# Group softmax: the last columns of three stores go out in ranges of partitions

One core of a Trainium2 chip. The metric is device time of the whole kernel in microseconds (us). Before the change it was 1326.43 us, the median of runs between 1326.30 and 1326.44.

## The reference

```python
def setup_inputs():
    B, N, D, G = 4, 4096, 4352, 8
    return {"x": np.random.randn(B, N, D).astype(np.float32)}

def reference(x):
    B, N, D = x.shape
    x_g = x.reshape(B, N, 8, D // 8)
    x_g = x_g - x_g.max(axis=-1, keepdims=True)
    exp = np.exp(x_g)
    return (exp / exp.sum(axis=-1, keepdims=True)).reshape(B, N, D)
```

285 MB are read and 285 MB written; there is little arithmetic for each byte.

## The kernel before

The input is cut into `nt` = 64 tiles of 128 partitions by 8704 columns of float32 (34,816 B per partition). There are six tile buffers. SyncE issues the loads. VectorE takes the maxima, ScalarE the exponentials and sums, VectorE multiplies by the reciprocals. GpSimdE issues the stores of tiles 0 to 61, SyncE the last two. A load of tile `t` waits until the store of tile `t - 6` has freed its buffer.

```python
    for t in range(nt):                                  # SyncE: loads
        if t >= NT:
            nc.sync.wait_ge(stored[t % NT], 16 * (t // NT))
        ...
            nc.sync.dma_start(out=tile_in[:, :], in_=xt[t]).then_inc(landed[t % NT], 16)
    ...
    for t in range(nt - LAST, nt):                       # SyncE: the last two stores
        nc.sync.wait_ge(scaled, t + 1 if t < nt - 1 else len(parts))
        nc.sync.dma_start(out=ot[t], in_=bufs[t % NT][:, :]).then_inc(last_stored, 16)

    for t in range(nt - LAST):                           # GpSimdE: all other stores
        nc.gpsimd.wait_ge(scaled, t + 1)
        nc.gpsimd.dma_start(out=ot[t], in_=bufs[t % NT][:, :]).then_inc(stored[t % NT], 16)
```

Of the kernel before, what the change touches and what calls it, by code (L numbers as in the profile page):

```python
# [1 line left out]

# [4 lines left out]


@with_exitstack
def kernel(  # L10
    ctx: ExitStack,
    tc: tile.TileContext,
    x: bass.AP,
    out: bass.AP,
):
    nc = tc.nc
    G = 8
    P = 128
    R = 2
    NT = 6  # L20
    RG = R * G
    xf = x.flatten_outer_dims()
    of = out.flatten_outer_dims()
    N, D = xf.shape
    Dg = D // G
    nt = N // (P * R)
    LAST = 2
    FIRST = 2
    turns = (nt - 1 - FIRST) // NT
    f32 = mybir.dt.float32  # L30
    X = mybir.AxisListType.X
    Exp = mybir.ActivationFunctionType.Exp
    xt = xf.rearrange("(t p r) d -> t p (r d)", p=P, r=R)
    ot = of.rearrange("(t p r) d -> t p (r d)", p=P, r=R)

    landed = [tc.alloc_semaphore(f"landed{b}") for b in range(NT)]
    stored = [tc.alloc_semaphore(f"stored{b}") for b in range(NT)]
    last_landed = tc.alloc_semaphore("last_landed")
    last_stored = tc.alloc_semaphore("last_stored")


    max_done = tc.alloc_semaphore("max_done")
    exp_done = tc.alloc_semaphore("exp_done")
    rec_done = tc.alloc_semaphore("rec_done")
    scaled = tc.alloc_semaphore("scaled")

    ctx.enter_context(tc.tile_critical(  # L47
        sync_engine=mybir.EngineType.Pool, no_gpsimd_drain=True))
    bufs = [ctx.enter_context(nc.sbuf_tensor(f"xt{b}", [P, R * D], f32)) for b in range(NT)]
    mx = ctx.enter_context(nc.sbuf_tensor("mx", [P, NT, RG], f32))  # L50
    sm = ctx.enter_context(nc.sbuf_tensor("sm", [P, NT, RG], f32))
    rs = ctx.enter_context(nc.sbuf_tensor("rs", [P, NT, RG], f32))

    parts = [(t, slice(0, RG)) for t in range(nt - 1)]
    parts += [(nt - 1, slice(r * G, (r + 1) * G)) for r in range(R)]

    def groups(t, g):
        return bufs[t % NT][:, :].rearrange("p (g d) -> p g d", d=Dg)[:, g, :]

    def vector_max(n):  # L60
        t, g = parts[n]
        i = nc.vector.reduce_max(  # L62
            out=mx[:, t % NT, g], in_=groups(t, g), axis=X, negate=True)
        if g.start == 0:
            i.wait_op(landed[t % NT], 16 * (t // NT + 1), "sem-ge")
        else:
            i.wait_op(last_landed, 16, "sem-ge")
        i.then_inc(max_done, 1)

    def vector_scale(n):  # L70
        t, g = parts[n]
        nc.vector.reciprocal(out=rs[:, t % NT, g], in_=sm[:, t % NT, g]).wait_op(  # L72
            exp_done, n + 1, "sem-ge").then_inc(rec_done, 1)
        xg = groups(t, g)
        nc.vector.tensor_tensor(  # L75
            out=xg,
            in0=xg,
            in1=rs[:, t % NT, g].unsqueeze(2).to_broadcast([P, g.stop - g.start, Dg]),
            op=mybir.AluOpType.mult,
        ).wait_op(rec_done, n + 1, "sem-ge").then_inc(scaled, 1)  # L80

    def scalar_exp(n, count):
        t, gs = parts[n]
        xg = groups(t, gs)
        for g in range(gs.start, gs.stop):
            i = nc.scalar.activation(  # L86
                out=xg[:, g - gs.start, :],
                in_=xg[:, g - gs.start, :],
                func=Exp,
                bias=mx[:, t % NT, g:g + 1],  # L90
                scale=1.0,
                accum_out=sm[:, t % NT, g:g + 1],
            )
            if g == gs.start:
                i.wait_op(max_done, count, "sem-ge")
        i.then_inc(exp_done, 1)



    for t in range(nt):  # L100
        if t >= NT:
            nc.sync.wait_ge(stored[t % NT], 16 * (t // NT))
        tile_in = bufs[t % NT]
        if t < nt - 1:
            nc.sync.dma_start(out=tile_in[:, :], in_=xt[t]).then_inc(landed[t % NT], 16)  # L105
        else:
            for r in range(R):
                nc.sync.dma_start(
                    out=tile_in[:, r * D:(r + 1) * D], in_=xt[t, :, r * D:(r + 1) * D],
                ).then_inc(landed[t % NT] if r < R - 1 else last_landed, 16)  # L110
    for t in range(nt - LAST, nt):
        nc.sync.wait_ge(scaled, t + 1 if t < nt - 1 else len(parts))
        nc.sync.dma_start(out=ot[t], in_=bufs[t % NT][:, :]).then_inc(last_stored, 16)


    for t in range(nt - LAST):
        nc.gpsimd.wait_ge(scaled, t + 1)
        nc.gpsimd.dma_start(out=ot[t], in_=bufs[t % NT][:, :]).then_inc(stored[t % NT], 16)  # L118
    for t in range(nt - NT, nt - LAST):
        nc.gpsimd.wait_ge(stored[t % NT], 16 * (t // NT + 1))  # L120
    nc.gpsimd.drain()
    nc.gpsimd.wait_ge(last_stored, 16 * LAST)

    nc.scalar.preload_act_table(Exp)  # L124

    for n in range(FIRST):
        scalar_exp(n, n + 1)
    nc.scalar.sem_inc(max_done, -FIRST)
    with nc.scalar.Fori(0, turns):
        for k in range(NT):  # L130
            scalar_exp(FIRST + k, k + 1)
        nc.scalar.sem_inc(max_done, -NT)
    for k, n in enumerate(range(FIRST + turns * NT, len(parts))):
        scalar_exp(n, k + 1)


    vector_max(0)
    for n in range(len(parts)):
        if n + 1 < len(parts):
            vector_max(n + 1)  # L140
        vector_scale(n)


# [1 line left out]
_INS = ['x']  # L145
_OUTS = [((4, 4096, 4352), 'float32')]


# [23 lines left out]
```

## Time and profile before

| | before |
|---|---|
| time, median | 1326.43 us |
| span of the profiled execution | 1324.7 us |
| share of 16 DMA engines held by the two queues | 51.5% + 48.3% |
| VectorE, ScalarE busy | 90%, 57% |

The prediction shows the lines and how they are read.

- **Mean and last landing.** The last store (tile 63) has 16 landings in the trace, one for each DMA engine (the packet records string into 16 chains, and in a chain a semaphore packet follows every eight rows of a whole store). The span is the mean of these 16 landings, plus the lag of the last behind the mean, plus 1.39 us, which is the same in the kernel before, the changed kernel and all experiments but two (e11 6.04, e12 9.43). Before: 1320.95 + 2.31 + 1.39 = 1324.65. Rebalancing can only reduce the 2.31.
- **Packets.** An undisturbed packet takes 36.8 ps per byte and 8 ns (1288 ns for 34,816 B).

### The profile page before, as it was taken

What the parts mean: (1) busy time and instruction counts of PE and PEld (TensorE: products, weight loads), DVE (VectorE), ACT (ScalarE), POOL (GpSimd) and SP (SyncE); (2) the same over time, 40 slices, a digit from 0 to 9 for tenths busy, and PEclk for the clock granted to TensorE, in tenths of its full rate; (3) what the DMA queues carried; (4) which work ended last, traced back from release to release, by engine and by line L of the source; (5) the groups of instructions that cost most, each with busy time, mean ns of one, the idle gap of its engine ahead of it and who ended that gap; (6) DMA issues with size and microseconds to landing.
All of it is one profiled execution on the core that took longest, in us unless ns stands there. A gap on an engine that the chain in (4) does not pass through costs nothing.

```text
span 1324.7 us, 2465 instructions
## 1 busy us (share of the span) xinstructions
DVE 1190.0 (90%) x195; ACT 757.4 (57%) x2049; POOL 33.3 (3%) x66
## 2 busy tenths in 40 slices
DVE  5999999988989889898898998988989889898893
ACT  3765566547456465564655646556465474654751
POOL 0000000000000000000000000000000000000000
DMA  9999999999999999999999999999999999999998
GB/s 404 421 434 433 432 432 434 434 432 431 435 435 432 430 434 437 432 432 432 436 434 430 433 435 433 431 433 435 433 433 431 434 436 432 431 432 437 432 432 372
DMA packets 18582, 570.48 MB, mean 431 GB/s; under 512 B 2064, under 2 KB 2064, under 8 KB 2064
## 3 DMA queue, kind: packets, MB, share of 16 engines
q1 hardware_dynamic: 9648, 294.13, 51.5%
q0 software_dynamic: 8928, 276.30, 48.3%
q14 instruction: 6, 0.05, 0.0%
HBM read 285.21 MB, written 285.21 MB: 431 GB/s over the span
## 4 chain that ended last, share of the span: by engine, by line
another core or an unknown queue 69%; DVE 20%; DMA 7%; ACT 1%; SPq 1%; issue 0%; POOLq 0%
DVE xt L75 10%; DVE mx L62 10%; DMA out_dram<-xt 4%; DMA xt<-in_x_dram 3%; ACT xt L86 1%; SPq L105 1%; DVE rs L72 0%; SPq L167 0%; POOLq L47 0%; POOLq L156 0%
## 5 line engine op out<-in xcount | busy, mean ns | idle before, releaser
L86 ACT ACTIVATE xt<-xt,mx 128x544 f32<-128x544 f32 x1024 | 750.1, 734 | 542.4 <-DVE mx L62 542.4
L62 DVE TENSOR_REDUCE mx<-xt 128x16 f32<-128x8704 f32 (+1 forms) x65 | 590.1, 9079 | 110.8 <-DMA xt<-in_x_dram 110.8
L75 DVE TENSOR_TENSOR xt<-xt,rs 128x8704 f32<-128x8704 f32 (+1 forms) x65 | 590.6, 9086 | 2.2
L86 ACT ACTIVATION_READ_ACCUMULATOR xt<-xt,mx 128x1 f32 x1024 | 191.6, 187 | 0.0
L118 POOL DMA_DIRECT2D out_dram<-xt x62 | 33.1, 534 | 1243.5 <-DVE xt L75 1243.5
L72 DVE RECIPROCAL rs<-sm 128x16 f32<-128x16 f32 (+1 forms) x65 | 15.7, 242 | 2.8 <-ACT xt L86 2.8
L124 ACT ACT_TABLE_LOAD x1 | 1.3, 1283 | 0.9 <-PEq L156 0.9
L156 POOL MEMSET const-float32-0.0<- 128x1 f32 x1 | 0.1, 98 | 0.2 <-issue 0.2
L156 POOL MEMSET const-bfloat16-1.0<- 128x1 bf16 x1 | 0.1, 101 | 0.0
L156 POOL MEMSET const-uint8-127<- 128x1 uint8 x1 | 0.1, 99 | 0.0
L156 POOL MEMSET const-float32-1.0<- 128x1 f32 x1 | 0.1, 98 | 0.0
## 6 DMA issues: line engine op xcount, KB each, us to landing
xt<-in_x_dram SPq DMA_DIRECT2D x63, 4352.0 KB, 32.4
out_dram<-xt POOLq DMA_DIRECT2D x62, 4352.0 KB, 51.5
out_dram<-xt SPq DMA_DIRECT2D x2, 4352.0 KB, 20.1
xt<-in_x_dram SPq DMA_DIRECT2D x2, 2176.0 KB, 35.1
```

What stands on the lines that cost most here:

```text
L62: i = nc.vector.reduce_max(out=mx[:, t % NT, g], in_=groups(t, g), axis=X, negate=True)
L72: nc.vector.reciprocal(out=rs[:, t % NT, g], in_=sm[:, t % NT, g]).wait_op(exp_done, n + 1, "sem-ge").then_inc(rec_done, 1)
L75: nc.vector.tensor_tensor(out=xg, in0=xg, in1=rs[:, t % NT, g].unsqueeze(2).to_broadcast([P, g.stop - g.start, Dg]), op=mybir.AluOpType.mu ...
L86: i = nc.scalar.activation(out=xg[:, g - gs.start, :], in_=xg[:, g - gs.start, :], func=Exp, bias=mx[:, t % NT, g:g + 1], scale=1.0, accum ...
L105: nc.sync.dma_start(out=tile_in[:, :], in_=xt[t]).then_inc(landed[t % NT], 16)
L118: nc.gpsimd.dma_start(out=ot[t], in_=bufs[t % NT][:, :]).then_inc(stored[t % NT], 16)
L124: nc.scalar.preload_act_table(Exp)
L156: nc = _bacc.Bacc("TRN2", target_bir_lowering=False, num_devices=1)
```

## The change

The intent, as its form tells it: take work from the DMA engine that ends last. In stores 24, 48 and 56 the last columns of all 128 rows are sent separately, in ranges of unequal numbers of partitions.

```diff
+    ranged = {24: (7344, [5, 105, 18]), 48: (7344, [8, 120]), 56: (8576, [48, 65, 15])}
+
+    def stores_of(t):
+        if t not in ranged:
+            return [(slice(0, P), slice(0, R * D))]
+        col, sizes = ranged[t]
+        dmas, p = [(slice(0, P), slice(0, col))], 0
+        for size in sizes:
+            dmas.append((slice(p, p + size), slice(col, R * D)))
+            p += size
+        assert p == P
+        return dmas
+
+    def stored_count(t):
+        return 16 * sum(len(stores_of(u)) for u in range(t % NT, t + 1, NT))
...
-            nc.sync.wait_ge(stored[t % NT], 16 * (t // NT))
+            nc.sync.wait_ge(stored[t % NT], stored_count(t - NT))
...
-        nc.gpsimd.dma_start(out=ot[t], in_=bufs[t % NT][:, :]).then_inc(stored[t % NT], 16)
+        for ps, cs in stores_of(t):
+            nc.gpsimd.dma_start(out=ot[t, ps, cs], in_=bufs[t % NT][ps, cs]).then_inc(
+                stored[t % NT], 16)
```

More of the change, by code (lines that the diff above doesn't have):

```diff
@@ L117 @@
         nc.gpsimd.wait_ge(scaled, t + 1)
-        nc.gpsimd.dma_start(out=ot[t], in_=bufs[t % NT][:, :]).then_inc(stored[t % NT], 16)
+        for ps, cs in stores_of(t):
+            nc.gpsimd.dma_start(out=ot[t, ps, cs], in_=bufs[t % NT][ps, cs]).then_inc(
+                stored[t % NT], 16)
     for t in range(nt - NT, nt - LAST):
-        nc.gpsimd.wait_ge(stored[t % NT], 16 * (t // NT + 1))
+        nc.gpsimd.wait_ge(stored[t % NT], stored_count(t))
     nc.gpsimd.drain()
```

## The prediction

> **What bounds the kernel now.** I read the page first: the busy shares, the DMA slices and the queues.
>
> ```profile
> DVE 1190.0 (90%) x195; ACT 757.4 (57%) x2049; POOL 33.3 (3%) x66
> DMA  9999999999999999999999999999999999999998
> GB/s 404 421 434 433 432 432 434 434 432 431 435 435 432 430 434 437 432 432 432 436 434 430 433 435 433 431 433 435 433 433 431 434 436 432 431 432 437 432 432 372
> q1 hardware_dynamic: 9648, 294.13, 51.5%
> q0 software_dynamic: 8928, 276.30, 48.3%
> ```
>
> VectorE has a tenth of its time free. The 16 DMA engines do not: the two queues hold 51.5 + 48.3 = 99.8% of their time, and only the first two slices and the last stand visibly below some 433 GB/s. Then the waits, of the engines and of SyncE's queue:
>
> ```profile
> DVE mx L62 <- DMA xt<-in_x_dram: 110.8, 51, 13.9
> SPq L105 <- DMA out_dram<-xt: 1201.7, 57, 67.8
> ```
>
> VectorE's waits are for loads; the loads' issuer waits for stores to free a buffer. Everything waits for transfers. The issues say how deep the transfers queue:
>
> ```profile
> xt<-in_x_dram SPq DMA_DIRECT2D x63, 4352.0 KB, 32.4
> out_dram<-xt POOLq DMA_DIRECT2D x62, 4352.0 KB, 51.5
> ```
>
> A tile's load and store together take some 20.6 us of all 16 engines (the pieces of the chain of waits come every 20.6 us). A load is under way for 32.4 us and a store for 51.5, so each engine always has packets of both waiting, and a late semaphore leaves no engine empty. Last, the end, in narrow stretches (columns: stretch, length, busy time of VectorE, ScalarE, GpSimdE, clock, DMA share, GB/s; a packet is counted where it starts):
>
> ```profile
> 1318.70:1320.00 1.30, 0.00 (x0) 0.00 (x0) 0.00 (x0) 1.00 0.74 321
> 1320.00:1320.60 0.60, 0.00 (x0) 0.00 (x0) 0.00 (x0) 1.00 0.14 58
> 1320.60:1321.50 0.90, 0.00 (x0) 0.00 (x0) 0.00 (x0) 1.00 0.18 77
> 1321.50:1322.00 0.50, 0.00 (x0) 0.00 (x0) 0.00 (x0) 1.00 0.00 0
> ```
>
> A packet is one row of 34,816 B. 58 GB/s over 0.60 us is one packet, 77 over 0.90 two. So three engines begin their last packet after the other 13, and the last of them ends the kernel.
>
> The trace's single packet records show more. On one engine a 34,816 B packet starts 1285 ns after the one before, so the packets can be strung into 16 chains. The chains end, in us from the span's start, at 1319.8 to 1320.8 (12 of them), 1321.1, 1321.3, **1322.2 and 1322.8**; the mean is 1320.6. The chain that is last (S1) loses a few ns on many packets: the last landing of a load falls behind the first by 2.2 us in mid-run and by 3.9 at the end, and from 600 us on the lag grows by 0.3 us every six tiles. The second (S2) was already a packet behind at 100 us, after a start in which the first packets took 1.8 to 2.4 us, and has one instruction fetch of 0.3 us. Were the bytes spread so that all chains ended together, the end would come 1322.8 - 1320.6 = 2.2 us earlier, 0.17%. **That is all that rebalancing can win.**
>
> [...]
> - [...] The trace before has only 128-partition stores, 16 landings each (62 x 16 + 67 x 16 = 2064)[...].
> - [...] in a chain q0 and q1 largely alternate.
> - [...] 16 x 34,816 B / 1285 ns = 433.5.
> - [...]
>
> **The change part by part.** No arithmetic, no load and no byte is taken away. Three of 62 stores (24, 48, 56) become one store of all rows' first columns plus two or three of the last columns. The tails are (8704 - 7344) x 4 = 5440 B per row in stores 24 and 48, (8704 - 8576) x 4 = 512 B in 56.
>
> [...]
>
> *The cost of a byte and a packet*: 34,816 B take 1285 ns and the 17,408 B packets of the last load 645 (start to start), so 36.8 ps per byte and 5 ns per packet. A semaphore packet adds some 6 ns.
> [...]
>
> *Beside it*: GpSimdE issues 8 more DMAs at 0.53 us (33.1 us for 62), 4.3 us, in an engine that waits 1243.5 us for VectorE: hidden. SyncE waits for 64 or 48 instead of 16 semaphore counts a little longer; the queues hide that.
>
> *The sum, if S1 is the relieved engine*: S1 ends at 1322.8 - 2.3 = 1320.5. S2 then sets the end, at 1322.2 + 0.2 to 0.4 = 1322.4 to 1322.6: a gain of only 0.2 to 0.4 us. If S2's early slip is this execution's accident, the next chain is 1321.3 + 0.4 = 1321.7: a gain of 1.1 us.
>
> **The rivals.**
> 1. *The relief misses* ([...]another slow engine in timed runs). For: nothing before shows an engine's number. Against: so exact a pattern must have been measured. The end moves by the +0.2 to +0.4 us that the others get: 1326.7.
> 2. [...] Tails of 24 and 48 are 8 x 5440 B x 36.8 ps = 1.6 us per engine each; a quarter to a half lost on both is +0.8 to +1.6 us, which cancels the gain: 1326.5 to 1328. For: the opening packets of up to 2.4 us[...]. Against: from there on almost all take 1288 ns, with loads and stores mixed.
> 3. *All lag goes*: both slow chains are nearer to the others in timed runs, and the whole 2.2 us less some 0.3 is won: 1324.5.
> 4. *A wait is lengthened*, loads start late and VectorE falls behind. At 20.6 us per tile it works 18.6, so it has 2 us a tile to catch up with, and the last calculation ends at 1306 us, some 15 before the last store. I give it next to nothing.
>
> **Range and chances.** The small gain 1326.43 - 0.3 = 1326.1 (weight 0.4), 1325.3 (0.25), the full 1324.5 (0.1), the miss 1326.7 (0.15), slower tails 1327.2 (0.1): the weighted mean is 1326.0; the care in the pattern makes me lean to its working, so 1325.8. The three runs before lie within 0.14 us, so noise adds little; 1324.5 to 1327.0. Two per cent would be 26.5 us, twelve times what rebalancing can win and more than the transfer of a whole tile: 1325.8 is as good as certain to be called same.
>
> **What would show it right or wrong.** Right: 62 + 8 = 70 stores from GpSimdE; 128 x 3 more data packets and 8 x 16 more semaphores, 18,582 + 512 = 19,094; under 2 KB 2064 + 256; GpSimdE busy some 37.6 us; DMA slices alike except the last; S1's chain back among the others and S2 last; packets of 5440 B in some 205 ns. Tails well over that, or slices 15 to 16 or 30 low, would be rival 2. A lone chain still at the end, later than before, would be rival 1. A time outside 1320 to 1335 would mean that a wait or a stall I have not seen took part.

The terms of the sum: -2.26 us for one relieved engine, taken to be S1's, and +0.19 to +0.40 us for the 15 others, from my assumption that successive ranges go round the engines ("rotation"). The sum came to S1 at 1322.8 - 2.3 = 1320.5 and S2, then the last, at 1322.4 to 1322.6, a gain of 0.2 to 0.4 us (1.1 if S2's slip was an accident); with the rivals weighed it gave 1325.8. "The +0.2 to +0.4 us that the others get" in rival 1 are the same terms. Rival 2 is "slower tails"; the quarter to a half lost there is a guess. The queues that largely alternate in a chain: from 300 to 500 us, 2776 of 2777 successive packets are of the other queue than the one before. The 433.5 is in GB/s: all 16 engines at one row in 1285 ns, against 430 to 437 in the full slices of the page.

## The result

1328.44 us (1327.97 to 1329.61 in four runs) against 1326.43: **2.0 us slower**, ratio 1.0017 with a 95% interval of 0.9999 to 1.0034, and outside the predicted range of 1324.5 to 1327.0. (Ratios are the mean time of one kernel's fast runs over that of the other's of the same rounds, so not quite the ratio of the medians quoted.) The profiled run is the fastest of the four (1327.97), so the profile can account for 1.5 of the 2.0 us.

Single runs must be read with care: in the later rounds, ten of 37 runs of the kernel before lie between 1327.0 and 1328.1. None of them was profiled. The change has no run under 1327.7 in eight (e8 included).

The page of the changed kernel, the lines that answer to those of before:

```profile
DVE 1189.7 (90%) x195; ACT 757.4 (57%) x2049; POOL 37.7 (3%) x74
DMA  9999999999999999999999999999999999999998
GB/s 403 420 437 436 435 425 435 436 435 433 428 436 434 437 432 428 433 434 428 433 434 434 434 433 433 432 436 435 431 433 434 434 419 435 432 433 433 431 434 373
DMA packets 19062, 570.48 MB, mean 430 GB/s; under 512 B 2244, under 2 KB 2275, under 8 KB 2544
q1 hardware_dynamic: 9648, 294.13, 51.5%
q0 software_dynamic: 9408, 276.30, 48.3%
L139 POOL DMA_DIRECT2D out_dram<-xt x70 | 37.5, 537 | 1238.6 <-DVE xt L95 1238.6
```

The engines are as full as before. In the GB/s line one slice stands out, the 33rd (1061 to 1094 us): 419, before 436. Store 48 is served there. Next, the waits of VectorE and of SyncE's queue:

```profile
DVE mx L82 <- DMA xt<-in_x_dram: 110.6, 48, 13.8
SPq L125 <- DMA out_dram<-xt: 1209.2, 57, 67.2
```

VectorE waits no longer than before (110.8 us), so nothing was lost on the compute side. And the end, in narrow stretches (columns as in the prediction):

```profile
1318.70:1320.00 1.30, 0.00 (x0) 0.00 (x0) 0.00 (x0) 1.00 0.99 429
1320.00:1320.60 0.60, 0.00 (x0) 0.00 (x0) 0.00 (x0) 1.00 1.07 464
1320.60:1321.50 0.90, 0.00 (x0) 0.00 (x0) 0.00 (x0) 1.00 0.45 193
1321.50:1322.00 0.50, 0.00 (x0) 0.00 (x0) 0.00 (x0) 1.00 0.49 209
1322.00:1323.00 1.00, 0.00 (x0) 0.00 (x0) 0.00 (x0) 1.00 0.16 70
1323.00:1323.50 0.50, 0.00 (x0) 0.00 (x0) 0.00 (x0) 1.00 0.16 70
```

Before, only two packets started after 1320.6. Now 193 GB/s x 0.90 us are 5 packets of 34,816 B, 209 x 0.50 are 3, then 2 and 1: eleven. It is not a single engine that ends later, **the whole crowd does**. The landings say so in numbers: the mean rose from 1320.95 to 1322.62 (+1.67), the lag of the last fell from 2.31 to 2.18 (-0.13): together the +1.5 us of the two spans. The 1.39 us after the last landing is the same in the kernel before, the changed kernel and all experiments but two (e11 6.04, e12 9.43).

Where did the mean go? The stretching around store 24 is 5.8 us, around store 48 16.0 (before: 0.2 and 0.2). After the first 60 us it sums to 1.94 us per engine, before to 0.32: **1.62 of the 1.67 us are stretched packets.** The page's columns show it around store 48. First the kernel before, then the changed one:

```profile
574.00:588.00 14.00, 12.00 (x4) 5.21 (x15) 0.53 (x1) 1.00 1.00 433
1068.00:1082.00 14.00, 11.99 (x4) 5.20 (x16) 0.53 (x1) 1.00 1.00 433
```

```profile
574.00:588.00 14.00, 13.97 (x4) 7.27 (x21) 0.53 (x1) 1.00 1.02 433
1068.00:1082.00 14.00, 13.97 (x4) 7.26 (x21) 0.53 (x1) 1.00 1.00 403
```

The busy share is the same 1.00 in the second stretch, but it moves 403 instead of 433 GB/s: busy, with longer packets. The 256 tail packets of 5440 B were not stretched: they took 208 ns, at most 227. The stretched ones are whole rows, loads for the most part, some 4 to 15 us after the tails.

One more difference shows in the timeline of SyncE's queue, the load of tile 30, which waits for store 24. Before, then changed:

```profile
565.94 0.33 SPq L105 DMA_DIRECT2D xt<-in_x_dram  x1
```

```profile
571.38 0.33 SPq L125 DMA_DIRECT2D xt<-in_x_dram  x1
```

It is issued 5.4 us later, and for some 6 us hardly any load packet is in service; the same happens at store 48. In the chains of the changed kernel tails and load packets alternate there (from 562.4 to 568 us, 113 of 120 successive packets are of the other queue): from 562.5 to 568 us it starts 34 tails and 60 load packets, e17 55 tails and 61 load packets. A tail of 205 ns uses up a turn like a row of 1285 ns, so in e17 the store queue moves 0.30 MB in tails there and the load queue 2.12 MB, and the split store lands late.

### The profile page after: what moved, and what is told of

It is laid out like the page before. It is cut to its first block, busy times and chain, and to the rows that moved or that the text cites. A ratio compares the mean times of both kernels' runs of the same rounds, so it can differ in the third digit from the quotient of the medians.

```text
span 1326.2 us, 2473 instructions
## 1 busy us (share of the span) xinstructions
DVE 1189.7 (90%) x195; ACT 757.4 (57%) x2049; POOL 37.7 (3%) x74
## 2 busy tenths in 40 slices
DMA packets 19062, 570.48 MB, mean 430 GB/s; under 512 B 2244, under 2 KB 2275, under 8 KB 2544
## 4 chain that ended last, share of the span: by engine, by line
another core or an unknown queue 69%; DVE 20%; DMA 7%; ACT 1%; SPq 1%; issue 0%; POOLq 0%
DVE xt L95 10%; DVE mx L82 10%; DMA out_dram<-xt 4%; DMA xt<-in_x_dram 3%; ACT xt L106 1%; SPq L125 1%; DVE rs L92 0%; SPq L189 0%; POOLq L67 0%; POOLq L178 0%
## 5 line engine op out<-in xcount | busy, mean ns | idle before, releaser
L139 POOL DMA_DIRECT2D out_dram<-xt x70 | 37.5, 537 | 1238.6 <-DVE xt L95 1238.6
```

Of the source, the lines that this page charges most:

```text
L139: nc.gpsimd.dma_start(out=ot[t, ps, cs], in_=bufs[t % NT][ps, cs]).then_inc(stored[t % NT], 16)
```

## The experiments

Three theories at the start. **A**: the late load, the dry load queue and its restart stretch the packets. **B**: rows sent in ranges of fewer than 128 partitions ("foreign" rows; "own" rows are those sent 128 at a time) stretch the packets. **C**: the relief went to the wrong engine. **D** came after the first runs: unequal numbers of packets take the engines out of step.

The names "own" and "foreign" come from my assumption that an engine then sends other rows. The traces show how many rows an engine sends, not which. Shares are called equal by what fits every count below, rows rounded up and always from the same engine; for e5, e6, e13 and e14 this is an estimate from those counts.

All kernels are the changed one with its table replaced by `pieces`, which lists for a tile the pieces of its store as (first partition, partitions, first column, end column); `W` = 8704. A tile that is not named is stored whole.

### First: no redistribution, ranges of 15 rows, small tails, a late load

```diff
# e1_uniform
+    pieces = {t: [(0, P, 0, 7344), (0, P, 7344, W)] for t in (24, 48)}
# e2_rotate
+    pieces = {t: [(p, min(15, P - p), 0, W) for p in range(0, P, 15)] for t in (24, 48)}
# e3_tail512
+    pieces = {t: [(0, P, 0, 8576), (0, P, 8576, W)] for t in (24, 48)}
# e4_late_load: no store is cut; in SyncE's loop
+            if t in (30, 54):
+                nc.sync.wait_ge(scaled, t - NT + 2)
```

> Stores 24 and 48 cut at column 7344 as in the change, but the tail is one 128-partition store: every engine keeps its 8 rows, nothing is moved between engines, store 56 is whole. Theory A (a tail packet of 5440 B takes a whole turn against a 34,816 B load packet, 8 extra turns of some 1.3 us per store, so the split store lands 5 to 7 us late, the next load is issued late, the load queue runs dry for some 6 us and the packets are stretched when it starts again): the loss stays though nothing is moved, load 30 issued at about 571.5 us instead of 565.9, load 54 at about 1066 instead of 1059.6, time 1327.5 to 1328.6. Theory B[...]: nothing of it is left here, 1326.4 to 1326.7 with loads 30 and 54 issued within 1 us of before. Theory C (the relief went to the wrong engine): also 1326.4 to 1326.7.

> Stores 24 and 48 in nine ranges of whole rows (eight of 15 partitions and one of 8), no column cut[...]. Theory A: no extra turns, loads 30 and 54 issued within 1 us of before, 1326.4 to 1326.8 (8 more semaphores per engine and store only). Theory B: [...] stretched packets in both stores, 1328 to 1332. Theory C: 1326.4 to 1326.8[...].

> As e1, but the cut is at column 8576, tails of 512 B. In the changed kernel the 512 B rows of one engine went as one packet (1536 and 2560 B), so 8 rows should be one packet of 4096 B and one extra turn instead of eight. Theory A: store lands under 1.5 us late, no dry stretch beyond that, 1326.4 to 1326.9. If instead the second semaphore wait or the second issue itself costs the time, it is as e1, 1327.5 to 1328.6.

> The kernel before with no store cut at all, but loads 30 and 54 also wait until the next tile is scaled, which makes their issue some 9 to 10 us late (574.8 and 1070 us). Theory A: a late load alone is enough: the load queue is dry for 8 to 11 us, packets are stretched after it, 1327 to 1329. If a late load is harmless and the small packets themselves cost the time, 1326.3 to 1326.6.

Measured: **e1** 1326.86 us, but its profiled run was one of 1335.44 (the other four 1326.77 to 1327.55; the kernel before 1326.60 in the same rounds). Load 30 was as late as theory A wanted (570.9 us) and the load queue dry for 5 us, yet the stretching around store 24 was 0.5 us. Around store 48 it was 5.6, and 49 in the whole of this bad run. **e2** 1360.26 us, 34 us slower, store packets of up to 6.0 us around store 24 and 9.3 around store 48: far over theory B's own range. **e3** 1326.66: no stretching (0.2 and 0.2), though load 30 came 2.5 us late, not under 1.5. **e4** 1326.46: a miss of mine. Tile 25 had been scaled long before, so the added wait never held anything back (load 30 at 564.5 us); it shows only that the wait itself is free.

What follows: A seemed to fall, B to stand, but e2 gives every theory a problem. Its nine ranges rest on the assumed rotation; without one they are not equal shares.

### Second: equal shares on foreign rows, one store alone, the change again

```diff
# e5_tail_112_16
+    pieces = {t: [(0, P, 0, 7344), (0, 112, 7344, W), (112, 16, 7344, W)] for t in (24, 48)}
# e6_rows_112_16
+    pieces = {t: [(0, 112, 0, W), (112, 16, 0, W)] for t in (24, 48)}
# e7_only48
+    pieces = {48: [(0, P, 0, 7344), (0, 8, 7344, W), (8, 120, 7344, W)]}
# e8_again: the three stores of the change, unaltered
```

> After the first four runs: late loads and extra turns are there in e1 and cost nothing in its undisturbed runs, so theory A has fallen[...]. Here stores 24 and 48 are cut at 7344 as in the change, the tails go in ranges of 112 and 16 partitions[...]. Theory B (foreign rows[...]): a loss as in the change, 1327.5 to 1329. Theory D (giving engines unequal numbers of packets takes them out of the step that they run in; loads then hinder each other until they have found a new one): nothing, 1326.6 to 1327.0 as e1.

> Stores 24 and 48 whole rows in ranges of 112 and 16 partitions[...], without small packets[...]. Theory B: stretched stores, less than in e2[...]; 1328 to 1345. Theory D: equal numbers of packets, 1326.4 to 1326.9.

> Only store 48 cut and spread as in the change. In the changed kernel the packets were stretched by some 0.3 us per engine after store 24 and by 1.0 after store 48. If the loss is the sum of such events, about two thirds of it are here: 1327.2 to 1328.0. [...] under theory C (the wrong engine is relieved) single runs should differ by up to 2 us, some under 1326.

> The changed kernel once more (same stores, ranges and columns, written as a table), to have it on the same chip as the others: 1327.9 to 1329.6 as recorded, all theories; a single value under 1326.5 would mean that the chip[...] decides.

Measured against 1326.57: **e8** 1328.02 (1327.74 to 1331.58) with stretching 6.4 and 15.0, nearly as in the first profile (5.8 and 16.0), so the pattern repeats. **e7** 1327.24 with 0.2 and 18.8: the stretching belongs to the store that is cut. Its runs spread over 2.1 us but none lies under 1326.6. **e6** 1339.08: foreign whole rows cost 12.5 us with equal shares, and store packets of up to 4.6 us. **e5** 1329.54, though its runs go from 1327.17 to 1332.22, and the profiled one (1327.96) has stretching of only 2.9 and 4.0 but a last engine 3.2 us behind the mean. For theory B too little stretching, for theory D too much time: e5 alone decides nothing.

### Third: ranges exchanged, other foreign rows, the change at the end, a marker

```diff
# e9_swapped: store 24 in (8, 120), store 48 in (5, 105, 18), store 56 as in the change
# e10_tail_64_64
+    pieces = {t: [(0, P, 0, 7344), (0, 64, 7344, W), (64, 64, 7344, W)] for t in (24, 48)}
# e11_at_end: the change's three tables at stores 59, 60, 61 in place of 24, 48, 56
# e12_marked: store 59 in pieces of 2, 3 and 15 partitions with widths of their own
+    for i, n in enumerate([2] * 8):
+        marked.append((p, n, 4000 + 64 * i))
+        p += n
+    ones = list(marked)
...
+    for i, n in enumerate([3, 2, 2, 2, 2, 2, 2, 2, 15]):
+        twos.append((p, n, 6000 + 64 * i))
+        p += n
+    pieces = {59: [(q, n, 0, c) for q, n, c in ones] + [(q, n, c, W) for q, n, c in ones]
+              + [(q, n, 0, c) for q, n, c in twos] + [(q, n, c, W) for q, n, c in twos]
+              + [(p, P - p, 0, W)]}
```

> Stores 24 and 48 exchange their ranges: store 24 gets 8 and 120 partitions, store 48 gets 5, 105 and 18. In the changed kernel and its repetition the packets are stretched by 4 to 6 us (sum over engines) around store 24 and by 15 to 16 around store 48. Theory D and theory B both say that it follows the ranges: some 15 us around 540 to 620 and 4 to 6 around 1035 to 1120. If it stays with the store (15 at 48), it comes from the state that the engines are in by then. Time in either case 1327.5 to 1328.6.

> Stores 24 and 48 cut at 7344, tails in two ranges of 64 partitions: 4 + 4 tails for every engine, equal[...]. Theory B: as much stretching as around store 48 of the change or more (10 us and up for each store), 1327.5 to 1329. Theory D: equal shares keep the step, 4 us or less for each store as in e5, 1326.6 to 1327.3.

> The same three sets of ranges in the same order, but in stores 59, 60 and 61, whose last columns go out after the last load has landed. Theory D: no load is left to be hindered and only some 40 us to be lost in, so the stretching is small (under 5 us in sum) and the mean of the engines' ends stays within 0.6 us of before. If the relieved engine is the last one of before, 1325.3 to 1326.3; if it is another one (theory C), 1326.5 to 1327.2.

> A marker, not a candidate: store 59 goes out in 35 pieces of 2, 3 or 15 partitions whose column counts differ[...]. It tells which engine is the last one at the end (the one that loses some ns on many packets) and whether it is[...] the one that the change relieves. Theory C: it is not. The time itself should be over 1328[...].

**e12 overturns the premise.** (It is a marker; its single run took 1374.22 us.) If the pieces rotated, eight pieces of 2 partitions would go to all 16 engines at nearly the same time. In the packet records each width occurs as two packets, and the widths follow one another:

```
bytes   start of its two packets, us
16000   1260.66  1261.53
16256   1262.55  1263.41
16512   1264.45  1265.31
16768   1265.72  1266.58
```

A packet of 16,000 B takes 596 ns and a load packet between them 1288: 1884 ns, and the next width comes 1.89 us later on both. The same two engines take one piece after the other. **There is no rotation in these runs: each piece begins with the same engine.** The changed kernel says so too. With its packets strung into 16 chains, the tails per chain of store 24 are

```
store 24   10 10 10 10 10  9  9  9  9  7  7  7  7  7  7  0
```

That is what 5 + 105 + 18 rows give if each range starts at the same engine: 1 + 7 + 2 on five, 7 + 2 on four, 7 on six, and **none on the sixteenth**. The sizes of store 56's tail packets show such shares directly: its 48, 65 and 15 rows of 512 B went as 16 packets of 1536 B, 13 of 2560 and 15 of 512, so 3, 5 and 1 rows to an engine. e9 has the exchanged ranges, and both of its stores count out exactly: 8 chains with 9, 7 with 8 and one with 0 for (8, 120), and the line above for (5, 105, 18). So the change relieves one engine of all 16 of its tails (16 x 5440 B x 36.8 ps = 3.2 us) and not another of twelve. Was that engine the last one? The slow engine, S1 of the prediction, is known by its packets of 1289 to 1310 ns where the others take 1288. When two packets end within some ns, chains cannot be told apart, so they were strung again with one more condition: an engine sends eight rows of a whole store or load and then its semaphore packet. In the best fits S1 has 10 tails of each (5, 105, 18) and 9 of each (8, 120), in all seven such stores of the change, e7, e8 and e9; the engine with none is another, ordinary one. **The relief missed the slow engine.** The lag of the last engine (2.18 and 2.05 us in the change's two profiles, 2.31 before) does not look relieved either.

**e10** 1328.06 us against 1326.47, stretching 14.4 and 13.5: every engine has 8 tails, and the loss is that of the change. As the sole cause, theory D falls. **e9** 1329.43: 19.0 us around store 24 and 13.0 around 48, so (8, 120) is costly at either store and (5, 105, 18) was not always cheap. **e11** 1330.75 (1328.64 to 1335.02), outside both ranges: the last load packets end at 1282 us, and still the store packets from 1270 to 1310 us are stretched, by 14 us in sum, the tails now too (242 ns on average, up to 782). The profiled run is the slowest, and much of its loss is something else: its span ends 6.04 us after the last landing, not 1.39. Moving the change to the end does not save it.

### Fourth: smaller ranges of whole rows, and is a late load enough?

```diff
# e13_rows_64_64
+    pieces = {t: [(0, 64, 0, W), (64, 64, 0, W)] for t in (24, 48)}
# e14_rows_16
+    pieces = {t: [(p, 16, 0, W) for p in range(0, P, 16)] for t in (24, 48)}
# e15_late_load: as e4, but
+                nc.sync.wait_ge(scaled, t - NT + 4)
# e16_tail512_64
+    pieces = {t: [(0, P, 0, 8576), (0, 64, 8576, W), (64, 64, 8576, W)] for t in (24, 48)}
```

> Stores 24 and 48 in two ranges of 64 partitions, whole rows[...]. [...] store packets of these stores of up to 2 x 1288 = 2576 ns,[...] 1330 to 1342. If sharing does not matter and only unequal shares do (theory D): 1326.4 to 1327.

> Stores 24 and 48 in eight ranges of 16 partitions, whole rows[...]. Theory B: store packets of up to 4 x 1288 = 5152 ns, a loss two to four times that of e13, 1345 to 1365, like e2 (which had up to 6.0 us[...]). Theory D: 1326.4 to 1327.

> e4 mended: loads 30 and 54 wait until the tile four after the stored one is scaled, some 9 to 10 us after their buffer is free (issue at about 574 and 1069 us). No store is cut. If a dry load queue alone is enough to stretch packets: 5 us or more in sum around 575 and 1070, 1327 to 1328.5. As e1 had dry stretches without loss I expect none: 1326.3 to 1326.8, apart from a chance run 1.3 us higher as the kernel before shows too.

> As e10, but the cut is at column 8576: foreign tails of 512 B, four of which go as one packet of 2048 B, so two extra turns per store in place of eight and hardly a dry load queue. If the foreign bytes count: a tenth of e10's, 1326.5 to 1326.9. If it is the mere presence of foreign rows that takes the engines out of step: as e10, 1327.5 to 1328.3.

The factors 2 and 4 on 1288 ns were my assumption that two and four engines hold each other up; no run shows that.

Against 1326.39: **e13** 1341.16 (+14.8; three runs, 1339.10 to 1347.64; a fourth, 1364.33, slow and left out), **e14** 1351.11 (+24.7). The stretching around store 24 is 31.6 us with 64 + 64 and 114.2 with ranges of 16. The same stretches of time (around stores 24 and 48) in the kernel before, e13 and e14:

```profile
540.00:580.00 40.00, 36.02 (x7) 23.63 (x64) 1.06 (x2) 1.00 1.01 434
1035.00:1085.00 50.00, 45.93 (x9) 27.42 (x75) 1.06 (x2) 1.00 1.00 433
```

```profile
540.00:580.00 40.00, 33.89 (x7) 23.63 (x64) 1.07 (x2) 1.00 1.00 411
1035.00:1085.00 50.00, 40.95 (x8) 27.79 (x76) 1.63 (x3) 1.00 1.00 400
```

```profile
540.00:580.00 40.00, 36.06 (x7) 23.63 (x64) 1.07 (x2) 1.00 1.00 366
1035.00:1085.00 50.00, 47.70 (x9) 32.27 (x87) 1.10 (x2) 1.00 1.01 407
```

The engines are always busy (share 1.00 to 1.01) and move 5 to 16% less. The order of e13 and e14 is theory B's. The median store packet around store 24 is still 1288 ns in both, so not every packet is slowed. What slows the others was not shown: the packet records that I used give times, queue and size, not the engine or the rows.

**e15** 1332.43, and I had expected nothing. Load 30 is issued at 575.3 us instead of 565.9:

```profile
575.33 0.33 SPq L124 DMA_DIRECT2D xt<-in_x_dram  x1
```

The stretching is not at the restart (1.8 us around store 24); it begins at 599 us and comes back with nearly every tile for 500 us, 6.5 us per engine in all. So a late load alone, with no store cut, can cost three times what the change does, in another pattern. Theory A is not dead as a mechanism, but what it makes is not what the change's trace has. **e16** 1327.30 (1326.38 to 1328.25; the kernel before also has a run of 1327.96 in these rounds), no stretching in its profile (0.2 and 0.3), which is of a run of 1326.79: there, foreign tails of a tenth of the bytes, in as many pieces as e10, do nothing visible. The median lies between the two expected ranges; what the runs of 1327.81 and 1328.25 hold is not known.

### Last: own against foreign rows, side by side

e17 is e1 again and e18 is e10 again, five rounds each on one chip.

> e1 again: stores 24 and 48 cut at 7344, one 128-partition tail, own rows. If own rows keep the packets unstretched: under 2 us in sum around 540 to 620 and around 1035 to 1120, loads 30 and 54 as late as in the change, most runs 1326.6 to 1327.0. If its disturbed run of before was the rule and not the exception, or the late load does it (as e15, 1332, suggests it can): 1328 and more in most runs.

> e10 again: the same cut, tails in two ranges of 64, equal shares, foreign rows. As e10: 12 to 15 us in sum around each of the two stores, 1327.8 to 1328.5 in most runs, so 1.0 to 1.5 us over e17 on the same chip. If own or foreign rows make no difference, it is as e17.

| kernel | median (range) of five runs, us | mean landing + lag, us | stretching at 24, 48 |
|---|---|---|---|
| before | 1326.39 (1326.31 to 1327.99, nine runs) | 1320.95 + 2.31 (first profile) | 0.2, 0.2 |
| e17, own rows | 1326.83 (1326.78 to 1326.97) | 1320.87 + 2.82 | 0.2, 0.2 |
| e18, foreign rows | 1328.01 (1327.77 to 1328.60) | 1322.71 + 1.89 | 14.9, 12.1 |
| the change | 1328.44 (1327.97 to 1329.61, four runs, other rounds) | 1322.62 + 2.18 | 5.8, 16.0 |

The same cut, the same shares, the same bytes; the loads for 24 and 48 are equally late. e17, then e18, the two stretches of 14 us again:

```profile
574.00:588.00 14.00, 13.97 (x4) 7.27 (x21) 0.53 (x1) 1.00 1.00 430
1068.00:1082.00 14.00, 13.97 (x3) 7.27 (x21) 0.02 (x1) 1.00 1.00 430
```

```profile
574.00:588.00 14.00, 13.97 (x4) 7.26 (x20) 0.53 (x1) 1.00 1.01 408
1068.00:1082.00 14.00, 13.97 (x4) 7.27 (x21) 0.53 (x1) 1.00 1.02 420
```

430 against 408 and 420 GB/s at the same busy share. The ranges of the two kernels' runs do not overlap: foreign rows cost 1.2 us at equal shares, and the cut with own rows 0.4. The change, with other ranges, costs 2.0. No kernel with a cut store beat the kernel before.

## Why the prediction was wrong, step by step

- **The bound** was right: the 16 DMA engines, to the end. VectorE's waits, GpSimdE's busy time (37.7 us, predicted 37.6) and the 70 stores are as worked out.
- **The cost of a byte and a packet** was right: 208 ns for 5440 B, which is 205 from start to start. The packet count came out at 19,062 for 19,094, because 512 B rows of one engine went together (1536 and 2560 B; 84 packets less) and 52 packets of 4 and 20 B came that I cannot account for.
- **Who gets which rows** was wrong. I had assumed that successive ranges go round the engines; e12 and the counts of e9 show no rotation. Shares of partitions rounded up fit every count: 5, 105 and 18 rows as 1, 7 and 2 to an engine, always from the same one. The argument "so exact a pattern must have been measured", by which I kept rival 1 at 0.15, was about the author, not about the chip. The engine relieved was not the slow one, so the relief missed, as rival 1 had it. The gain of 0.2 to 1.1 us did not come: the lag fell by 0.13 us.
- **The sum left stretching at zero**, and this step cost the most: instead of a small gain, the mean landing rose by 1.67 us. Stretching was 1.62 us per engine. Rival 2 had the size right (0.8 to 1.6 us) and the wrong weight (0.1), and its own check, "tails well over 205 ns", would have cleared it: the tails took 208 and whole rows after them were stretched. e17 against e18 shows that foreign rows bring it (0.2 and 0.2 us against 14.9 and 12.1); e10 shows that unequal shares are not needed.
- **"The queues hide that"** (the longer wait for the split store) was half right. The load was 5.4 us late and its queue ran dry. With own rows the medians rose by only 0.3 and 0.4 us (e1, e17), with one bad run in ten, 1335.44; but e15 shows that two late loads, the first by 9.4 us, cost 6.
- **Left open.** Why unstretched foreign tails are followed by stretched loads 4 to 15 us later, why (5, 105, 18) brought 6 us of stretching at store 24 and 13 at store 48, and what keeps e15 and the one bad run of e1 stretched for hundreds of us.

## What to carry to other kernels

With the DMA engines full all the time, as here (99.8%), the last engine's lag was all that rebalancing could win (2.3 of 1325 us), while the disturbance was paid by all of them (each of the 16 landings, in their order, at least 1.1 us later, the mean 1.67): compare the mean landing as well as the last. Store 128 partitions at a time; here cutting columns cost little (0.4 us for two stores), cutting partitions more even when the shares stayed equal (1.6 us). And before work is steered to single engines, mark the packets with sizes of their own and see where they go.
